# A two-layer diffusion backbone on one core: projections for query, key and value over 512 weight columns at a time, and layer 0's key scores for all x tokens in one pass

## The chip, the cores and the metric

The kernel runs on one core of a Trainium2 chip. The metric is the time of one execution on the device in microseconds (us). The kernel before takes 5148.17 us (median of three runs, 5141.2 to 5151.72).

## What is computed

There are 512 latent tokens (x) and 256 context tokens (ctx), 1024 channels, two layers. Cut to what matters here, each layer does this:

```python
p = xn @ wl                              # one input projection, 10 x 1024 columns; ctx likewise
q = rope(rms(p[..., Q] per 64 columns))  # 8 heads x 2 x 64
k = rope(rms(p[..., K] per 64 columns)); v = p[..., V]
o = softmax(q0 k0) v - lam * softmax(q1 k1) v      # over 768 keys: x and ctx
mix = (g0*rms(o) + g1*pool(p) + g2*conv(p) @ conv_out_w) @ w_out ; h = h + mod*mix
s = (xn2 @ w_q) against 16 tables of 128 keys      # PEER: 8 heads x 2 halves
eidx, gate = top 16 of the sums of two top-16 lists, softmax over them
h = h + mod * sum_k gate*gelu(xn2 . u_emb[eidx]) * v_emb[eidx]   # 128 experts per token
```

Layer 1 needs only the x tokens at its end.

## The kernel before, in words

Every product of two float32 arrays is made of three matmuls in float32r (`mm3`, L96 to L100): both sides are split into a high and a low part (`split`, L91 to L94: a copy on ACT, a subtraction on DVE). Names in the profile: `whi` and `wlo` are the split weights, `hi` and `lo` (or `yh`, `yl` before the FFN) the split activations.

**Projections.** `load_w` (L136) fetches a weight chunk of 1024 x 256 in two DMAs of 512 KB (`wraw`), splits each, and `qkv` (L298) runs, for each pair of heads and each of k, q and v, over token tiles: two token tiles of 256 columns fill one PSUM bank (`qk`), and `qk_tile` normalizes, rotates, splits, transposes and stores them. The token tile is the stationary side of the matmul, the weight columns are what moves. There are 9 chunks of two token tiles for each pair of heads in layer 0 and 8 in layer 1.

**Mixers.** `conv`, `conv_gate`, `conv_out` and `out_proj` run with the weight as the stationary side over 512 tokens. `attn_gate` broadcasts a row of 1/rms to all partitions by a matmul with a selector (`selb`, `hrb`, L494), in float32.

**The FFN has two ways.** For the 512 x tokens of layer 0 (384 in layer 1) all 16384 experts are computed: `keys` scores (`mm<-yh`, `rsc`) and picks the top 16 (MAX8, FIND_INDEX8 and MATCH_REPLACE8 on DVE, `tv`, `ti`, `mr`), `gates` builds a dense gate array (`gA`, `gE`, `gB`, `gps`), `hidden` multiplies by all of u (`ul`, `hid`: 24 matmuls of 512 columns for each split weight tile `ul`, 128 such tiles) and `values` by all of v (`vl`, `dps`). For the 256 ctx tokens of layer 0 (and 128 x tokens of layer 1) `gathered` (L841) fetches the 128 chosen rows of `peer_u` and of `peer_v` for each of 128 tokens by indirect DMAs issued by POOL, 128 x 1024 floats (512 KB) each, into **three buffers** (`row`); DVE multiplies each row (L859, with a sum into `ghid`) or accumulates it (L869, `gacc`). That is 512 rows in layer 0 and 256 in layer 1. Their priority is the lowest of all.

**Order.** The framework's scheduler writes one fixed order of instructions for each engine; each engine then runs its list in that order, and a wait holds up all that is behind it. DVE's list mixes the gathered rows with the splits (`wlo`, `ul`, `vl`) for which TensorE waits. `keys` is called in layer 0 and 1 for two halves of the x tokens, the later half first, which lets the second half's picks start before the first half is scored.

Of the kernel before, what the change touches and what calls it, by code (L numbers as in the profile page):

```python
# [21 lines left out]
F32 = mybir.dt.float32  # L22
# [47 lines left out]
class Net:  # L70
# [227 lines left out]

    def qkv(self, l, streams, kinds):

        nc, a = self.nc, self.a
        with ExitStack() as es:
            ap_ = self.pool(es, f"at{l}{streams[0].i}", 2)
# [3 lines left out]
            for hp in range(NH // 2):  # L307
                for kind in kinds:
                    w = self.load_w(a["w_in"][l, {"q": 0, "k": 4, "v": 8}[kind] + hp], KT, 256)
                    for s in streams:  # L310
                        if l == DEPTH - 1 and s.i and kind == "q":
                            continue
                        for u in range(s.nt // 2):
                            ps = pm.tile([P, 2, 256], F32, tag="mm", name="qk")
                            for t in range(2):
                                for k in range(KT):
                                    xh, xl = s.sub(k, 2 * u + t)
                                    self.mm3(ps[:, t], xh, xl, w[0][k], w[1][k], k == 0, k == KT - 1)
                            if kind == "v":
                                vh = ap_.tile([P, 2, 2, P], F32R, tag="vh", name="vh")  # L320
                                vl = ap_.tile([P, 2, 2, P], F32R, tag="vl", name="vl")
                                pv = ps.rearrange("p t (h c) -> p h t c", h=2)
                                self.split(vh, vl, pv)
                                t0 = (s.t0 + 2 * u) * P
                                for x, v in enumerate((vh, vl)):
                                    for hh in range(2):
                                        nc.scalar.dma_start(self.vd[l][x, 2 * hp + hh][:, t0:t0 + 2 * P],
                                                          v[:, hh].bitcast(F32).rearrange("p t c -> p (t c)"))
                            else:
                                self.qk_tile(l, ap_, pt_, "qk".index(kind), hp, s, u, ps, rot)  # L330

    def qk_tile(self, l, ap_, pt_, i, hp, s, u, ps, rot):
# [3 lines left out]
        psg = ps.rearrange("p t (g c) -> p (t g) c", c=HD)  # L336
# [9 lines left out]
        y4 = y.rearrange("p (t g) c -> p t g c", t=2)  # L346
        z4 = z.rearrange("p (t g) c -> p t g c", t=2)
        if s.i == 0:
            t1 = ap_.tile([P, 8, HD], F32, tag="qt", name="qt")
            t4 = t1.rearrange("p (t g) c -> p t g c", t=2)  # L350
            cx = rc[:, i, 2 * u:2 * u + 2]
            sx = rs[:, i, 2 * u:2 * u + 2]
            nc.vector.tensor_tensor(z4, y4, cx[:, :, None].to_broadcast([P, 2, 4, HD]), op=OP.mult)
            for a_, b_ in ((0, 32), (32, 0)):
                nc.vector.tensor_tensor(t4[:, :, :, a_:a_ + 32], y4[:, :, :, b_:b_ + 32],
                                        sx[:, :, None, a_:a_ + 32].to_broadcast([P, 2, 4, 32]), op=OP.mult)
# [3 lines left out]
        o = (s.t0 + 2 * u) * P  # L360
        st = ap_.tile([P, 2, 2, 2 * P], F32R, tag="st", name="st")
        if i == 0:
# [6 lines left out]
            blk = lambda t, g: zz[:, 2 * t + g // 2, 2 * (g % 2):2 * (g % 2) + 2]  # L369
        else:  # L370
# [5 lines left out]
            blk = lambda t, g: zz[:, 4 * t + g]  # L376
        for t in range(2):
            tr = pt_.tile([P, 4, P], F32R, tag="tr", name="tr")
            for g in range(4):
                nc.tensor.transpose(tr[:, g], blk(t, g).rearrange("p a c -> p (a c)"), self.identr)  # L380
            nc.scalar.activation(st[:, :, :, t * P:(t + 1) * P].rearrange("p h i c -> p (h i) c"), tr, AF.Copy)
        dst = (self.qd, self.kd)[i][l]
        for hh in range(2):
            nc.scalar.dma_start(dst[2 * hp + hh][:, :, o:o + 2 * P], st[:, hh].bitcast(F32))
        if i == 1:
            sl = ap_.tile([P, 2, 2 * P], F32R, tag="sl", name="sl")
            tr = pt_.tile([P, 4, P], F32R, tag="tr", name="tr")
            for hh in range(2):
                for t in range(2):
                    nc.tensor.transpose(tr[:, 2 * hh + t], kl[:, 4 * t + 2 * hh:4 * t + 2 * hh + 2].rearrange("p a c -> p (a c)"), self.identr)  # L390
            nc.scalar.activation(sl.rearrange("p h c -> p (h c)"), tr.rearrange("p a c -> p (a c)"), AF.Copy)
            for hh in range(2):
                nc.scalar.dma_start(self.ld[l][2 * hp + hh][:, o:o + 2 * P], sl[:, hh].bitcast(F32))
# [64 lines left out]
    def attn_gate(self, l, s, pp):  # L458

        nc, a = self.nc, self.a  # L460
        with ExitStack() as es:
# [6 lines left out]
            selb = gp.tile([NH, NH, P], F32, name="selb", bufs=1)  # L468
# [3 lines left out]
            def gate(c):  # L472
                w = self.load_w(a["w_in"][l, 28 + c], KT, 256)
# [14 lines left out]
            R = self.rsqrt_wide(gp, ss, 1.0 / P, [NH, s.n], "hr")  # L488
            for j in range(NH):
# [4 lines left out]
                nc.tensor.matmul(rb, selb[:, j], R, start=True, stop=True)  # L494
# [717 lines left out]
```

## Time and profile before

| | |
|---|---|
| median of three runs | 5148.17 us |
| the profiled execution, its own time | 5138.01 us |
| its span, first to last instruction | 5136.2 us |
| TensorE (PE) busy | 4934.7 us, 96% |
| VectorE (DVE) busy | 3946.9 us, 77% |
| ScalarE (ACT) busy | 1988.4 us, 39% |
| bytes moved | 1280.77 MB, 249 GB/s over the span |

Busy PE time is a union of spans that overlap, since one matmul's span is longer than the distance to the next one's start; how fast PE works is read from the number of matmuls in a stretch. The profiled execution is 10 us shorter than the median of the runs, 1.8 us of its time lie outside the span.

### The profile page before, as it was taken

The numbers are of one execution on the slowest core, as the hardware profiler recorded it, in microseconds if no ns is written. First come the engines' busy times: TensorE is split into PE (matmuls) and PEld (weight loads), VectorE is DVE, ScalarE is ACT, GpSimd is POOL, SyncE is SP. The second block draws the span as 40 slices with busy tenths as digits, with TensorE's granted clock in tenths as the row PEclk, the third lists the DMA queues.
The fourth block names the chain that finished last, engine by engine and source line by source line (L and its number), as shares of the span: only waits on it lengthen the run. The fifth ranks groups of instructions, "written<-read, shape, count | busy, mean of one in ns | idle before, by whom it ended". The sixth has DMA issues, their size and how long they took to land.

```text
span 5136.2 us, 73940 instructions
## 1 busy us (share of the span) xinstructions
PE 4934.7 (96%) x27373; PEld 4195.8 (82%) x27373; DVE 3946.9 (77%) x7993; ACT 1988.4 (39%) x2968; POOL 1180.5 (23%) x1028
## 2 busy tenths in 40 slices
PE   8999999998899999989999999999999999899999
PEld 5688787776688788768888789777679999899999
DVE  5457676697899998568888867666359999787885
ACT  4346664422333344222233234544334344332333
POOL 0001000024433343333333300000000434344320
PEclk9999999999999999999999999999999999999999
DMA  8667453468897889999999845533355888988995
GB/s 305 239 200 224 137 191 108 155 200 273 302 316 259 285 312 339 329 321 326 336 341 344 311 137 166 161 126 97 109 172 174 277 309 331 330 314 294 329 317 177
DMA packets 509035, 1280.77 MB, mean 249 GB/s; under 512 B 42496, under 2 KB 224640, under 8 KB 500352
## 3 DMA queue, kind: packets, MB, share of 16 engines
q1 hardware_dynamic: 302816, 669.35, 38.5%
q0 software_dynamic: 131968, 449.90, 25.7%
q10 hardware_dynamic: 73888, 156.79, 8.1%
q8 instruction: 215, 3.52, 0.3%
q14 instruction: 148, 1.21, 0.1%
HBM read 1098.13 MB, written 177.73 MB: 248 GB/s over the span
## 4 chain that ended last, share of the span: by engine, by line
PE 64%; DMA 14%; DVE 11%; issue 7%; POOL 2%; ACT 1%; SPq 0%; ACTq 0%; POOLq 0%; DVEq 0%
PE mm L98 6%; DMA row<-peer_v,ix 6%; PE mm L100 6%; PE mm L99 6%; DMA row<-peer_u,ix 6%; PE dps L99 5%; PE dps L100 5%; PE dps L98 5%; PE hid L100 4%; PE hid L98 4%; PE hid L99 4%; PE qk L98 3%; PE qk L100 3%; PE qk L99 2%; POOL row L846 2%
## 5 line engine op out<-in xcount | busy, mean ns | idle before, releaser
L100 PE MATMUL hid<-yh,ul 128*128 128x512 f32 (+1 forms) x2048 | 760.2, 372 | 33.9 <-DVE ul L94 33.6
L98 PE MATMUL hid<-yh,uh 128*128 128x512 f32 (+1 forms) x2048 | 757.1, 370 | 21.0 <-ACT yh L286 13.2
L846 POOL DMA_INDIRECT row<-peer_v,ix x384 | 568.5, 1480 | 876.7 <-DVE gacc L869 501.1
L846 POOL DMA_INDIRECT row<-peer_u,ix x384 | 521.4, 1358 | 1059.7 <-DVE row L859 617.7
L99 PE MATMUL hid<-yl,uh 128*128 128x512 f32 (+1 forms) x2048 | 755.7, 369 | 2.3 <-DVE yl L287 2.3
L98 PE MATMUL dps<-wh,vh 128*128 128x512 f32 (+1 forms) x2048 | 735.1, 365 | 20.0 <-ACT vh L93 18.6
L99 PE MATMUL dps<-wl,vh 128*128 128x512 f32 (+1 forms) x2048 | 741.7, 365 | 12.3 <-DVE wl L94 12.3
L100 PE MATMUL dps<-wh,vl 128*128 128x512 f32 (+1 forms) x2048 | 742.0, 364 | 10.4 <-DVE vl L94 10.4
L98 PE MATMUL mm<-hi,whi 128*128 128x512 f32 (+1 forms) x1856 | 666.5, 360 | 12.3 <-DVE y L582 3.1
L100 PE MATMUL mm<-hi,wlo 128*128 128x512 f32 (+1 forms) x1856 | 660.6, 358 | 14.0 <-DVE wlo L94 14.0
L99 PE MATMUL mm<-lo,whi 128*128 128x512 f32 (+1 forms) x1856 | 662.4, 357 | 3.5 <-DVE lo L94 3.5
L859 DVE SCALAR_TENSOR_TENSOR row<-row,gx 128x1024 f32<-128x1024 f32 x384 | 467.0, 1221 | 170.3 <-DMA row<-peer_u,ix 169.5
L869 DVE SCALAR_TENSOR_TENSOR gacc<-row,gw,gacc 128x1024 f32<-128x1024 f32 x381 | 488.1, 1281 | 133.7 <-DMA row<-peer_v,ix 132.6
L94 DVE TENSOR_TENSOR wlo<-wraw,whi 128x1024 fp32r<-128x1024 f32 (+1 forms) x356 | 427.2, 1202 | 179.6 <-ACT whi L93 177.2
L93 ACT ACTIVATE uh<-uraw 128x1024 fp32r<-128x1024 f32 x256 | 271.5, 1061 | 716.4 <-PE hid L99 651.9
L93 ACT ACTIVATE whi<-wraw 128x1024 fp32r<-128x1024 f32 (+1 forms) x356 | 370.5, 1043 | 404.4 <-PE mm L99 305.2
L93 ACT ACTIVATE vh<-vraw 128x1024 fp32r<-128x1024 f32 x256 | 270.2, 1058 | 641.9 <-PE dps L99 395.1
L100 PEld LDWEIGHTS hid<-yh,ul 128*128 128x128 f32 x2048 | 390.2, 191 | 82.9 <-DVE ul L94 44.6
L98 PEld LDWEIGHTS hid<-yh,uh 128*128 128x128 f32 x2048 | 391.1, 191 | 64.1 <-ACT yh L286 15.6
L98 PEld LDWEIGHTS dps<-wh,vh 128*128 128x128 f32 x2048 | 386.7, 189 | 61.9 <-ACT vh L93 19.4
L99 PEld LDWEIGHTS dps<-wl,vh 128*128 128x128 f32 x2048 | 387.1, 189 | 54.8 <-DVE wl L94 14.4
L100 PEld LDWEIGHTS dps<-wh,vl 128*128 128x128 f32 x2048 | 387.2, 189 | 51.5 <-DVE vl L94 11.1
(332 smaller groups left out, 9480.4 us busy)
## 6 DMA issues: line engine op xcount, KB each, us to landing
uraw<-uT SPq DMA_DIRECT2D x256, 512.0 KB, 5.7
vraw<-v SPq DMA_DIRECT2D x256, 512.0 KB, 6.8
wraw<-w_in SPq DMA_DIRECT2D x216, 512.0 KB, 4.4
gd<-gst ACTq DMA_DIRECT2D x28, 2048.0 KB, 10.7
mw<-w_mod SPq DMA_DIRECT2D x96, 512.0 KB, 7.0
wraw<-wq SPq DMA_DIRECT2D x80, 512.0 KB, 6.0
hidd<-ge ACTq DMA_DIRECT2D x128, 256.0 KB, 5.6
G<-gd SPq DMA_DIRECT2D x32, 1024.0 KB, 10.7
```

Source lines behind the costliest of these rows:

```text
L93: self.nc.scalar.activation(hi, src, AF.Copy)
L94: self.nc.vector.tensor_tensor(lo, src, hi.bitcast(F32), op=OP.subtract)
L98: mm(ps, lh, rh, start=start, stop=False)
L99: mm(ps, lh, rl, start=False, stop=False)
L100: mm(ps, ll, rh, start=False, stop=stop)
L846: nc.gpsimd.indirect_dma_start(out=r, out_offset=None, in_=a[t], in_offset=bass.IndirectOffsetOnAxis(ap=idx[:, s:s + 1], axis=0))
L859: nc.vector.scalar_tensor_tensor(out=r, in0=r, scalar=1.0, in1=x, op0=OP.mult, op1=OP.mult, accum_out=hid[:, k:k + 1])
L869: nc.vector.scalar_tensor_tensor(acc, r, w[:, k:k + 1], acc, op0=OP.mult, op1=OP.add)
```

## The change

Four things change.

1. `qkv` takes weight chunks of 1024 x 512 (four heads). `load_wide` fetches one in four DMAs of 512 KB, and its split tiles alternate between a pool of their own (`wq`, three buffers) and the shared one. One token tile of 512 columns now fills a PSUM bank, with 24 matmuls of 512 columns instead of 48 of 256 for two token tiles of half the width. What `qk_tile` computes for a bank is as much as before; the stores of a pair of token tiles are merged into two DMAs (three for k).
2. Layer 0 calls `keys` once for all 512 x tokens. Layer 1 still calls it twice.
3. `attn_gate` splits the 1/rms row and broadcasts it by two float32r matmuls in place of one in float32.
4. The weight array is cut differently in memory (`w_qkv` beside `w_in`), so chunk numbers shift.

```diff
+    def load_wide(self, src, wq):
+        hi, lo = [], []
+        for k0 in range(0, KT, 2):
+            raw = self.wpool.tile([P, 2, 512], F32, tag="wraw", name="wraw", bufs=3)
+            self.nc.sync.dma_start(raw, src[:, k0 * 512:(k0 + 2) * 512].rearrange("p (k c) -> p k c", c=512))
+            pool, n = (wq, 3) if k0 // 2 % 2 else (self.wpool, self.wbufs)
+            h = pool.tile([P, 2, 512], F32R, tag="whi", name="whi", bufs=n)
+            lw = pool.tile([P, 2, 512], F32R, tag="wlo", name="wlo", bufs=n)
+            self.split(h, lw, raw)
...
-            for hp in range(NH // 2):
+            for hg in range(2):
...
-                    w = self.load_w(a["w_in"][l, {"q": 0, "k": 4, "v": 8}[kind] + hp], KT, 256)
+                    w = self.load_wide(a["w_qkv"][l, {"q": 0, "k": 2, "v": 4}[kind] + hg], wq)
...
-                            ps = pm.tile([P, 2, 256], F32, tag="mm", name="qk")
                             for t in range(2):
+                                ps = pm.tile([P, 512], F32, tag="mm", name="qk")
                                 for k in range(KT):
                                     xh, xl = s.sub(k, 2 * u + t)
-                                    self.mm3(ps[:, t], xh, xl, w[0][k], w[1][k], k == 0, k == KT - 1)
+                                    self.mm3(ps, xh, xl, w[0][k], w[1][k], k == 0, k == KT - 1)
...
+            rh = gp.tile([NH, s.n], F32R, name="hrh", bufs=1)
+            rl = gp.tile([NH, s.n], F32R, name="hrl", bufs=1)
+            self.split(rh, rl, R)
...
-                nc.tensor.matmul(rb, selb[:, j], R, start=True, stop=True)
+                nc.tensor.matmul(rb, selb[:, j], rh, start=True, stop=False)
+                nc.tensor.matmul(rb, selb[:, j], rl, start=False, stop=True)
...
-                for t0 in (XT // 2, 0):
-                    y = Stream(0, XT // 2 * P, 0)
-                    y.h, y.l = (x[:, :, t0 * P:t0 * P + y.n] for x in (Y.h, Y.l))
+                for t0, t1 in ((XT // 2, XT), (0, XT // 2)) if l else ((0, XT),):
+                    y = Stream(0, (t1 - t0) * P, 0)
+                    y.h, y.l = (x[:, :, t0 * P:t1 * P] for x in (Y.h, Y.l))
```

The scheduler writes a new order for the whole program. Three places follow, all in DVE's list of layer 0.

The first is where `conv` of the x tokens begins (`z` is its first product). In the kernel before, DVE still picks experts for ctx there:

```order
L94 TENSOR_TENSOR wlo<-wraw,whi 128x1024
L687 TENSOR_SCALAR ri<-pos 128x128
L688 TENSOR_SCALAR ci<-pos 128x128
L679 TENSOR_REDUCE gz<-ge 128x8
L572 TENSOR_TENSOR z<-mm,z 128x512
L630 MAX top<-cand 128x8 x8
L691 CAST rf<-ri 128x128
L692 CAST cf<-ci 128x128
L680 RECIPROCAL gz<-gz 128x8
L572 TENSOR_TENSOR z<-mm,z 128x512
```

In the changed kernel the gathered rows are already running at the same place:

```order
L94 TENSOR_TENSOR wlo<-wraw,whi 128x1024
L872 SCALAR_TENSOR_TENSOR row,ghid<-row,gx 128x1024
L726 TENSOR_TENSOR pk_10969<-eq 128x128
L872 SCALAR_TENSOR_TENSOR row,ghid<-row,gx 128x1024 x2
L94 TENSOR_TENSOR wlo<-wraw,whi 128x1024
L1025 SCALAR_TENSOR_TENSOR ix_10971<-pk_10961,pk_10969 128x128
L585 TENSOR_TENSOR z<-mm,z 128x512 x2
L872 SCALAR_TENSOR_TENSOR row,ghid<-row,gx 128x1024
L94 TENSOR_TENSOR wlo<-wraw,whi 128x1024
L588 SCALAR_TENSOR_TENSOR y<-z,cols,y 128x512 x2
```

The gather moved ahead: it starts 14 weight splits (`wlo`) earlier than it did.

The second is where the x tokens are scored, with `hidden` already running beside it. Before, from one `ul` to the next:

```order
L94 TENSOR_TENSOR ul<-uraw,uh 128x1024
L869 SCALAR_TENSOR_TENSOR gacc<-row,gw,gacc 128x1024
L634 MAX tv_14967<-mr 128x8
L635 MAX_INDEX ti_14970<-tv_14966,mr 128x8
L709 TENSOR_TENSOR eq<-eq,tf 128x2048
L631 MAX_INDEX ti_14970<-tv_14966,rsc 128x8
L634 MAX top<-mr 128x8 x2
L630 MAX tv_14967<-rsc 128x8
L869 SCALAR_TENSOR_TENSOR gacc<-row,gw,gacc 128x1024
L635 MAX_INDEX ti_14971<-tv_14967,mr 128x8
L633 MATCH_REPLACE mr<-tv_14966,rsc 128x128
L711 TENSOR_TENSOR eq<-eq 128x1024
```

And in the changed kernel, up to the next `ul`:

```order
L872 SCALAR_TENSOR_TENSOR row,ghid<-row,gx 128x1024
L644 MAX_INDEX ti_14022<-tv_14018,rsc 128x8
L646 MATCH_REPLACE mr<-tv_14018,rsc 128x128
L872 SCALAR_TENSOR_TENSOR row,ghid<-row,gx 128x1024
L647 MAX tv_14017<-mr 128x8
L647 MAX tv_14018<-mr 128x8
L872 SCALAR_TENSOR_TENSOR row,ghid<-row,gx 128x1024
L648 MAX_INDEX ti_14021<-tv_14017,mr 128x8
L648 MAX_INDEX ti_14022<-tv_14018,mr 128x8
L643 MAX tv_14019<-rsc 128x8
L94 TENSOR_TENSOR ul<-uraw,uh 128x1024
L872 SCALAR_TENSOR_TENSOR row,ghid<-row,gx 128x1024
```

The rows stand closer, and the picks (`eq`, `top`) that stood among the scores of the second half are gone from here; they now come after all scores. Counted over DVE's whole list, the gathered rows stand like this (before, now): between the 143rd and the 192nd `wlo` 93, 123; between the 10th and the 28th `ul` 40, 68; from there to the 46th 36, 36; from there to the last 127, 120; and in `values`, between the 16th and the 88th `vl`, 111, 111. TensorE's list for the 18 `ul` from the 10th holds 192 `mm` of 512 columns and 36 `rsc` besides the 432 `hid` matmuls now, and for the 18 after them next to nothing else. The picks for ctx, on which the gather waits, now lie ahead of the 143rd `wlo`.

The third is the end of layer 0. Before, the last tile of the gather (`gres`) closes the layer, just ahead of the next layer's norm (`nrm`):

```order
L875 SCALAR_TENSOR_TENSOR gres<-gtr,modT_98,gres 128x128
L831 TENSOR_TENSOR acc<-dps,acc 128x512
L835 SCALAR_TENSOR_TENSOR acc<-acc,modT_98,fh 128x512
L875 SCALAR_TENSOR_TENSOR gres<-gtr,modT_98,gres 128x128 x2
L94 TENSOR_TENSOR wlo<-wraw,whi 128x1024 x3
L123 TENSOR_SCALAR nrm<-nps 128x512
L127 TENSOR_TENSOR nrt<-nry 128x256 x2
```

In the changed kernel it is done some 36 of the 128 `vl` earlier:

```order
L844 TENSOR_TENSOR acc<-dps,acc 128x512
L848 SCALAR_TENSOR_TENSOR acc<-acc,modT_98,fh 128x512
L94 TENSOR_TENSOR wlo<-wraw,whi 128x1024 x2
L123 TENSOR_SCALAR nrm<-nps 128x512
L123 TENSOR_SCALAR nrm<-nps 128x256
L127 TENSOR_TENSOR nrt<-nry 128x256 x2
```

What moved is the whole gather of layer 0, towards its start. Layer 1's lists after its projections differ in a few places only.

## Rows read from the trace of the kernel before

**Rows 1.** The page: engines' busy time, and engines on the chain that ended last.
```profile
PE 4934.7 (96%) x27373; PEld 4195.8 (82%) x27373; DVE 3946.9 (77%) x7993; ACT 1988.4 (39%) x2968; POOL 1180.5 (23%) x1028
...
PE 64%; DMA 14%; DVE 11%; issue 7%; POOL 2%; ACT 1%; SPq 0%; ACTq 0%; POOLq 0%; DVEq 0%
```

**Rows 2.** Timeline of PE in layer 0's projections: start, span.
```profile
144.07 0.28 PE L100 MATMUL qk<-whi,lo 128*128 128x256 f32 x1
144.19 0.28 PE L98 MATMUL qk<-whi,hi 128*128 128x256 f32 x1
...
146.11 0.28 PE L99 MATMUL qk<-wlo,hi 128*128 128x256 f32 x1
```

**Rows 3.** Stretch table of tile `dps` alone: stretch, length, PE, PEld, DVE; clock, DMA, GB/s.
```profile
2515.00:2580.00 65.00, 65.00 (x289) 53.83 (x288) 8.61 (x13) 1.00 0.98 341
```

**Rows 4.** Stretch table, values: PE, PEld, DVE, ACT, POOL busy; clock, DMA share, GB/s.
```profile
2305.00:2925.00 620.00, 620.00 (x2735) 513.17 (x2734) 543.62 (x720) 183.22 (x232) 229.51 (x172) 1.00 0.96 336
```

**Rows 5.** The same table from the x mixers to the end of `hidden`.
```profile
1000.50:1087.90 87.40, 87.40 (x427) 71.67 (x426) 82.26 (x338) 24.88 (x32) 6.71 (x10) 1.00 0.33 109
1087.90:1362.90 275.00, 235.56 (x954) 182.18 (x953) 212.79 (x279) 78.19 (x98) 122.58 (x103) 0.95 0.82 281
...
1453.40:1605.40 152.00, 148.80 (x824) 129.14 (x823) 145.39 (x494) 53.45 (x71) 42.09 (x40) 0.99 0.85 288
1605.40:1734.70 129.30, 120.27 (x644) 98.64 (x644) 119.53 (x315) 39.08 (x64) 53.63 (x38) 0.99 0.80 269
1734.70:2253.10 518.40, 509.24 (x2894) 416.08 (x2894) 414.58 (x646) 193.51 (x297) 192.51 (x124) 0.99 0.90 322
```

**Rows 6.** Two of these stretches, tile `row` alone: DVE, then POOL's issues.
```profile
1087.90:1362.90 275.00, 116.00 (x141) 120.10 (x94) 0.95 0.82 281
...
1453.40:1605.40 152.00, 50.29 (x56) 42.09 (x40) 0.99 0.85 288
```

**Rows 7.** Tile `row` from 1085 to 1345: instructions (min/median/max ns), landing.
```profile
L859 DVE SCALAR_TENSOR_TENSOR row<-row,gx x48: 1209/1224/1278, 1092.1 to 1317.5; 128x1024 f32<-128x1024 f32 x48
...
DMA to landing us min/median/max: 4.4/6.2/9.4
```

**Rows 8.** Who waited for whom, 1085 to 1345: total, times, longest.
```profile
POOL row L846 <- DVE row L859: 61.4, 39, 3.9
...
DVE row L859 <- DMA row<-peer_u,ix: 30.0, 21, 2.9
...
PE mm L100 <- DVE wlo L94: 13.5, 9, 3.2
```

**Rows 9.** Groups of PE by shape: count, busy, mean ns, idle before.
```profile
L98 PE MATMUL qk<-whi,hi 128*128 128x256 f32 x1088 | 312.5, 288 | 5.6 <-DVE qy L344 2.2 <-ACT hi L286 1.9 <-DVE nt L285 1.6
...
L98 PE MATMUL mm<-yh,whi 128*128 128x256 f32 x512 | 147.3, 288 | 0.0
...
L494 PE MATMUL hrb<-hry,selb 8*128 8x512 f32 x32 | 18.4, 700 | 4.1 <-DVE hry L133 4.1
...
L494 PE MATMUL hrb<-hry,selb 8*128 8x256 f32 x16 | 6.3, 490 | 1.2 <-ACT rg L476 1.2
```

**Rows 10.** The stretch table in the projections of layers 0 and 1.
```profile
0.00:384.00 384.00, 367.08 (x2522) 266.28 (x2522) 205.36 (x600) 146.27 (x233) 13.22 (x46) 0.99 0.72 249
...
3066.00:3196.00 130.00, 130.00 (x1119) 130.00 (x1119) 91.64 (x271) 54.24 (x78) 0.00 (x0) 1.00 0.47 153
```

**Rows 11.** Chain that ended last, between layers: start, length, what.
```profile
2986.80 1.72 PE nps L275 x4
...
2990.09 3.99 DMA hout<-gres
2994.13 4.74 DMA h<-hout
...
2999.36 2.09 PE nps L275 x4
...
3007.90 0.58 PE qk L98
```

More of the change, by code (lines that the diff above doesn't have):

```diff
@@ L296, in norm @@
                 nc.scalar.dma_start(rows.rearrange("(q p) d -> p q d", p=P), nrow)
+    def load_wide(self, src, wq):
[7 more added lines that the diff above has]
+            self.split(h, lw, raw)
+            for k in range(2):
+                hi.append(h[:, k])
+                lo.append(lw[:, k])
+        return hi, lo
     def qkv(self, l, streams, kinds):
@@ L302, in qkv @@
         with ExitStack() as es:
+            wq = self.pool(es, f"wq{l}{streams[0].i}")
             ap_ = self.pool(es, f"at{l}{streams[0].i}", 2)
@@ L313, in qkv @@
                         for u in range(s.nt // 2):
-                            ps = pm.tile([P, 2, 256], F32, tag="mm", name="qk")
+                            c = slice((s.t0 + 2 * u) * P, (s.t0 + 2 * u + 2) * P)
+                            st = ap_.tile([P, 2, 4, 2, P], F32R, tag="st", name="st")
+                            sl = ap_.tile([P, 4, 2, P], F32R, tag="sl", name="sl") if kind == "k" else None
                             for t in range(2):
+                                ps = pm.tile([P, 512], F32, tag="mm", name="qk")
@@ L316, in qkv @@
                                 for k in range(KT):
                                     xh, xl = s.sub(k, 2 * u + t)
-                                    self.mm3(ps[:, t], xh, xl, w[0][k], w[1][k], k == 0, k == KT - 1)
[L319 to L330, printed above, removed]
@@ L332, in qk_tile @@
-    def qk_tile(self, l, ap_, pt_, i, hp, s, u, ps, rot):
+                                    self.mm3(ps, xh, xl, w[0][k], w[1][k], k == 0, k == KT - 1)
+                                if kind == "v":
+                                    self.split(st[:, 0, :, t], st[:, 1, :, t], ps.rearrange("p (h c) -> p h c", h=4))
+                                else:
+                                    self.qk_tile(l, ap_, pt_, "qk".index(kind), s, 2 * u + t, t, ps, rot, st, sl)
+                            for x in range(2):
+                                src = st[:, x].bitcast(F32).rearrange("p h t c -> p h (t c)")
+                                if kind == "v":
+                                    dst = self.vd[l][x, H][:, :, c]
+                                else:
+                                    dst = (self.qd, self.kd)["qk".index(kind)][l][H][:, :, x, c]
+                                nc.scalar.dma_start(dst.rearrange("h p c -> p h c"), src)
@@ L334, in qk_tile @@
+                            if kind == "k":
+                                nc.scalar.dma_start(self.ld[l][H][:, :, c].rearrange("h p c -> p h c"),
+                                                    sl.bitcast(F32).rearrange("p h t c -> p h (t c)"))
+    def qk_tile(self, l, ap_, pt_, i, s, u, t, ps, rot, st, sl):
         nc = self.nc
         rc, rs, gains = rot
-        psg = ps.rearrange("p t (g c) -> p (t g) c", c=HD)
+        psg = ps.rearrange("p (g c) -> p g c", c=HD)
         sq = ap_.tile([P, 8, HD], F32, tag="qt", name="sq")
@@ L375, in qk_tile @@
             nc.vector.tensor_tensor(kl, z, zz[:, :, 0].bitcast(F32), op=OP.subtract)
-            blk = lambda t, g: zz[:, 4 * t + g]
-        for t in range(2):
+            blk = lambda h, x: zz[:, 2 * h + x]
+        for x in range(2):
             tr = pt_.tile([P, 4, P], F32R, tag="tr", name="tr")
[L379 to L384, printed above, removed]
+            for h in range(4):
+                nc.tensor.transpose(tr[:, h], blk(h, x).rearrange("p a c -> p (a c)"), self.identr)
+            nc.scalar.activation(st[:, x, :, t], tr, AF.Copy)
         if i == 1:
-            sl = ap_.tile([P, 2, 2 * P], F32R, tag="sl", name="sl")
             tr = pt_.tile([P, 4, P], F32R, tag="tr", name="tr")
[L388 to L393, printed above, removed]
+            for h in range(4):
+                nc.tensor.transpose(tr[:, h], kl[:, 2 * h:2 * h + 2].rearrange("p a c -> p (a c)"), self.identr)
+            nc.scalar.activation(sl[:, :, t], tr, AF.Copy)
     def attend(self, l, es, parts, side=None):
@@ L1170, in layouts @@
     r["w_mod"] = chunk(I["w_mod"], 12, KT, 512)
-    r["w_in"] = chunk(I["w_in"], 40, KT, 256)
+    r["w_qkv"] = chunk(I["w_in"][:, :, :3 * D], 6, KT, 512)
+    r["w_in"] = chunk(I["w_in"][:, :, 3 * D:], 28, KT, 256)
     r["conv_out_w"] = chunk(I["conv_out_w"], 4, KT, 256)
```

32 lines of the change are left out of this document (13 added, 19 removed).

## The prediction

> **What bounds the kernel now.** I read the page first. TensorE is busy for 96% of the span, but the chain of waits gives only 64% to it and 14% to DMA, 11% to VectorE [rows 1]. Busy time overlaps itself, so I counted how far apart matmuls start. In the projections 18 matmuls of 256 columns start from 144.07 to 146.11: 2.04 / 17 = 0.120 us each [rows 2]. A matmul of 512 columns takes 65.00 / 289 = 0.225 us [rows 3], and 620.0 / 2735 = 0.227 over the whole values stage, where TensorE never pauses [rows 4]; I use 0.2265. So a pair of 256 costs 0.240, and one of 512 saves 13.5 ns against it.
>
> Where TensorE does pause decides the rest. The stretch table has one bad place: from 1087.9 to 1362.9 TensorE is busy for 235.6 of 275 us [rows 5]. There the gather's rows pass: DVE multiplies 94 of them, one in 275 / 94 = 2.93 us, and POOL's issues of them are in that stretch too [rows 6]. A row takes 1.22 us on DVE and lands 6.2 us (median, 9.4 at most) after its issue [rows 7]. POOL waits for DVE to free a buffer 39 times, 61.4 us in all, DVE waits for a landing 30.0 us, and TensorE waits for `wlo`, which stands behind such rows in DVE's list [rows 8]. Three buffers share one cycle of landing and multiplication, so rows have a pace of their own: (6.2 + 1.22) / 3 = 2.47 us if nothing lies between them, 2.93 as measured with all hand-offs. I take 2.8, nearer to what was measured, because issue and semaphores do cost something. **A stretch whose list holds n rows lasts at least 2.8 n, whatever TensorE has to do.**
>
> **The change, part by part.**
>
> *Projections.* 1088 matmuls per line, three lines, of 256 columns [rows 9]: 3264 x 0.120 = 391.7 us. Now 1632 x 0.2265 = 369.6: -22. In layer 1 TensorE works without a pause and DVE and ACT are busy 91.6 and 54.2 of 130 us [rows 10], their work for a bank is the same, so the gain comes through. In layer 0 TensorE works 367 of 384 us with DMA at 0.72 [rows 10]; a wait could take some of it. I take -21, between 0 (only if each weight chunk, now twice as large, is late by what it saved) and -22.
>
> *Stores and weights.* I cost them at nothing. A bank's 24 matmuls last 5.4 us, in which ACT works 54.24 x 5.4 / 130 = 2.3 us and DVE 3.8 [rows 10]; the merged stores are issued from ACT in the 3.1 us that are left, and bytes and copies per bank stay as they are. Weights come as often per column as before, four tiles for a chunk that lasts twice as long, on SP's queue with nothing else in front. If that cover went, each of the 12 chunks of the two layers would make TensorE wait for one split, 1.2 us of DVE, 15 us in all, which is most of the bound of 0 above.
>
> *Broadcast.* 48 records of `hrb` in float32 take 18.4 + 6.3 us [rows 9]; as 32 matmuls of 512 and 16 of 256 in float32r at the spacings above, 7.2 + 1.9. That is -15.6, of which up to two thirds can be hidden or eaten by the split that now stands ahead of it (one copy and one subtraction for each gate, TensorE behind them): the x gate of layer 0 lies where the rows set the pace. I take -5, from 0 to -11.
>
> *Keys.* 768 of the 1536 `mm` matmuls of 256 columns [rows 9] become 384 of 512: 92.2 to 87.0 us. It lies in the stretches below and is counted there, as are the 16 weight chunks that are no longer fetched and split twice. What matters more is what the new order does with the gather, since DVE's list is fixed and each row in it holds up `ul` and `wlo` behind it.
>
> *x mixers, 143rd to 192nd `wlo`.* Now 87.4 + 275.0 = 362.4 us [rows 5] with 93 rows; 123 in the new list: 123 x 2.8 = 344. The picks for ctx, with which DVE is busy 82.3 of the first 87.4 us now [rows 5], stand ahead; I let the list come about a quarter of them late, 22 us. 344 + 22 - 362 = +4. Bounds: -18 without the lateness, +20 at 2.93 us.
>
> *10th to 28th `ul`.* Now 152.0 us [rows 5] with 40 rows, 42.1 us of POOL's time [rows 6]. The new list has 68: 68 x 2.8 = 190, against what TensorE needs there, (432 + 192) x 0.2265 = 141 and 36 small `rsc`, 148 in all. So the rows set the end: +38. Bounds: -4 (TensorE alone), +47 at 2.93.
>
> *28th to 46th `ul`.* Now 129.3 us [rows 5]. The second half's scores and picks are gone; 432 x 0.2265 = 98 for TensorE and near 100 with what little else is there, 36 x 2.8 = 101 for the rows: -28. Bounds -29 and -24.
>
> *Rest of `hidden`.* Work doesn't vanish: TensorE is busy 148.8 + 120.3 = 269 us in the two stretches now [rows 5], needs 148 + 98 then, and the keys account for 5 of the difference. Some 16 us (gates that come later) move into this rest, which is busy 509 of 518 [rows 5], at fewer rows (127 to 120): +8, from 0 to +16.
>
> *Values.* 111 rows before and after over the same 72 `vl`, one in 3.6 us (620 / 172) [rows 4], DMA share 0.96, TensorE without a pause: 0. Only the last 36 `vl` lose their rows, and nothing waited for those.
>
> *Between the layers.* The chain runs through `hout<-gres`, 3.99 us, and `h<-hout`, 4.74 us, after the last `nps` of x [rows 11]. With `gres` long done, both can leave the chain. I take -5 (ctx's norm must still pass behind something), from 0 to -9.
>
> **Sum**, against the profiled execution's own 5138.0 us: -21 - 5 + 4 + 38 - 28 + 8 + 0 - 5 = -9, 5129. The median of the runs is 10 us above that execution, so 5139 on its scale; I say 5140. A measurement of this kernel can tell some 0.2%, 10 us, from no change: below 5138 counts as faster, above 5158 as slower.
>
> The size of the bets: of the +38 and +4, 2.8 us is the uncertain factor. Each 0.1 us on it moves the total by some 20 us.
>
> **Rivals.**
>
> *B, the rows do not hold up `ul` or `wlo`.* Their pace is 2.6 us or less. For it: landing was 4.4 us at best [rows 7], and a longer `ul` stretch spreads its weight fetches thinner. At 2.6: x mixers 320 + 22 - 362 = -20, `ul` 177 - 152 = +25, then -29: -21 - 5 - 20 + 25 - 29 + 8 - 5 = -47, 5101 on the median's scale; down to 5080 if the pace never shows. Against it: [rows 6] and [rows 8] show this very limit, with TensorE at 86%.
>
> The Trainium skill, "DMA: Bandwidth & Descriptors", section "Anatomy of one DMA — SWDGE (gpsimd) path", gives 2.0 us plus bytes over 436e3, an estimate of 3.2 us for such a row of 512 KB. By that the cycle would be (3.2 + 1.22) / 3 = 1.5 us and this rival would hold. The landings of 4.4 to 9.4 us in [rows 7] do not agree with it.
>
> *C, slower: the denser list runs at 2.93 us or above.* The `ul` stretch fetches weights beside the rows (DMA 0.85 with 40 rows [rows 5]); with 68 the landing could rise above its 6.2 us. At 2.93: +20, +47, -24 in place of +4, +38, -28, so 29 more in all, 5169; at 3.1: +41, +59, -17, so 5209. It decides at about 2.9. Against it: the longer stretch spreads the same weight fetches, so its bytes per us need not rise; and 2.93 had the x mixers' waits in it.
>
> *D, the wide matmul isn't cheaper than its two halves.* Then -21 and the 5 of the keys are gone: 5140 + 26 = 5166. Against it are the two spacings that I read directly [rows 2, 3]; for it, only that no 512-column `qk` is in the trace.
>
> The Trainium skill, "TensorE: Matmul & The Clock Gate", section "Back-to-back issue gap", speaks against the change: its isolated gap is N / 2.4 + 2.5 ns, so two of 256 cost 218.3 and one of 512 costs 215.8, only 2.5 ns saved and, as an estimate, 4 us over 1632 matmuls. By that the sum would be 5161 (17 and 4 of the two savings gone). The trace's 0.120 and 0.2265 [rows 2, 3] differ from it by 10 ns each, which is a saving of 13.5.
>
> **How the numbers follow.** A, as forecast, pace 2.7 to 2.9: 0.45, with 5120 to 5165; of that 0.20 falls below 5138, 0.17 within, 0.08 above. B, 0.28, all faster. C, 0.20, and D, 0.07, slower. So faster 0.48, same 0.17, slower 0.35. The range of 8 in 10 reaches into B (5097) and into C (5188).
>
> **What would show it.** Projections right: TensorE's `qk` at 0.226 us spacing, 544 records per line instead of 1088, and layer 1's projections 10 us shorter. Gather right: from the 10th to the 28th `ul` some 190 us with TensorE idle a fifth of it, waiting for `ul` on DVE, and POOL waiting for DVE's rows; 28th to 46th near 100 us. If that first stretch takes 150 us, B; if 205, C. Between the layers: no `hout<-gres` on the chain. The forecast fails if rows are limited otherwise than by three buffers, or if the picks that moved ahead hold up TensorE before the 143rd `wlo`, which I priced at 22 us of lateness only.

## The result

The changed kernel is **slower**: 5226.15 us median (5222.99 to 5249.43) against 5149.86 us for the kernel before, ratio 1.0161, interval 1.0130 to 1.0193. The prediction said 5140 us and a range up to 5188. The profiled execution has a span of 5221.2 us, 85.0 more than before.

The page of the changed kernel, the lines that answer to [rows 1]:

```profile
PE 4939.3 (95%) x25357; PEld 4094.2 (78%) x25357; DVE 3934.8 (75%) x7980; ACT 1974.2 (38%) x2941; POOL 1142.4 (22%) x1028
...
PE 24%; issue 7%; DMA 4%; DVE 4%; POOL 1%; ACT 1%; POOLq 0%; DVEq 0%; ACTq 0%
```

The shares of this chain add up to 41% of the span, so the profile does not follow it back to the start, and they can't be set beside the 64% of before.

TensorE is as busy as before although it has 2016 fewer matmul records: what it saved is filled with longer spans and lower clocks, and with pauses. The busy share hides all of this; the stretches show it. Each stage below runs from the end of the one above to the first start of a tile or, where it says "last", to the end of that tile's last matmul, in us of one profiled execution of each kernel:

| stretch | before | changed | difference | forecast |
|---|---|---|---|---|
| start to last `qk`, layer 0 | 367.6 | 344.0 | -23.6 | -11 |
| to the first `ul` (all mixers) | 967.4 | 1034.5 | **+67.1** | +4, and part of -5 |
| 1st to 10th `ul` | 118.4 | 114.9 | -3.5 | 0 |
| 10th to 28th | 152.0 | 186.1 | **+34.1** | +38 |
| 28th to 46th | 129.3 | 115.8 | -13.5 | -28 |
| 46th to 128th | 526.0 | 528.3 | +2.3 | +8 |
| to the last `dps`, layer 0 | 726.1 | 722.8 | -3.3 | 0 |
| to the first `qk`, layer 1 | 21.1 | 17.8 | -3.3 | -5 |
| first to last `qk`, layer 1 | 209.7 | 219.5 | **+9.8** | -10 |
| to the first `hid`, layer 1 | 606.2 | 614.6 | +8.4 | part of -5 |
| to the end | 1312.4 | 1322.9 | +10.5 | 0 |

The largest loss lies in the mixers, where the x gate begins. The stretch table of the changed kernel there (PE, PEld, DVE, ACT, POOL; clock, DMA share, GB/s), which answers to the first row of [rows 5]:

```profile
980.00:1000.00 20.00, 14.06 (x63) 8.02 (x61) 19.45 (x127) 4.73 (x8) 2.36 (x10) 0.83 0.01 3
1000.00:1020.00 20.00, 6.07 (x8) 0.80 (x8) 20.00 (x123) 4.71 (x8) 0.00 (x0) 0.68 0.00 0
1020.00:1040.00 20.00, 18.78 (x63) 13.51 (x64) 17.38 (x53) 6.71 (x8) 7.70 (x5) 0.81 0.29 83
1040.00:1060.00 20.00, 15.65 (x57) 11.13 (x57) 19.30 (x30) 3.21 (x4) 7.79 (x6) 0.87 0.93 325
```

And who waited for whom from 980 to 1060 (total, times, longest):

```profile
POOL row L859 <- DVE gg L695: 43.3, 1, 43.3
...
PE hrb L506 <- ACT hrh L93: 9.4, 1, 9.4
ACT osq L495 <- PE hss L496: 9.2, 4, 5.5
```

From 1000 to 1020 DVE works without a pause through 123 small instructions, the picks for ctx, while TensorE has 8 matmuls and the DMA engines nothing. The granted clock falls to 0.68, a mean of 20 us at its two levels (1.2 and 2.4 GHz), after those pauses. In the kernel before TensorE is busy for all of 87.4 us there.

The stall is one part of the loss. The two lines below are the changed kernel, from the 143rd `wlo` to the first gathered row and from there to the first `ul`; the two after them are the same stretches of the kernel before:

```profile
980.00:1036.10 56.10, 35.30 (x121) 19.89 (x120) 52.97 (x293) 14.61 (x22) 8.91 (x13) 0.76 0.05 14
1036.10:1378.50 342.40, 301.56 (x1226) 234.97 (x1224) 262.69 (x341) 85.66 (x107) 152.16 (x135) 0.96 0.84 287
```

```profile
1000.50:1092.10 91.60, 91.60 (x445) 75.13 (x444) 83.53 (x340) 25.61 (x33) 9.55 (x14) 1.00 0.35 117
1092.10:1335.00 242.90, 213.79 (x890) 168.32 (x888) 186.61 (x242) 64.43 (x80) 107.62 (x93) 0.98 0.83 282
```

TensorE stands still for 20.8 us of the first stretch, where it did not pause before. In the second it stands still for 40.8 us instead of 29.1, and the stretch is 99.5 us longer: 118 rows pass there instead of 85, and matmuls that covered the picks before are done there (1226 records instead of 890).

Elsewhere: the gathered rows in the mixers and in two `ul` stretches (tile `row` alone: DVE, then POOL's issues), then all instructions of the `ul` stretches:

```profile
1100.00:1360.00 260.00, 116.15 (x141) 116.42 (x93) 0.97 0.83 282
1493.40:1679.50 186.10, 85.15 (x100) 71.20 (x68) 0.98 0.85 282
1679.50:1795.30 115.80, 44.75 (x54) 40.14 (x36) 0.99 0.87 291
```

```profile
1493.40:1679.50 186.10, 164.53 (x714) 128.73 (x713) 156.85 (x435) 39.76 (x53) 71.20 (x68) 0.98 0.85 282
1679.50:1795.30 115.80, 106.58 (x466) 86.44 (x465) 104.23 (x338) 33.31 (x44) 41.68 (x37) 0.99 0.87 291
```

The first `ul` stretch holds 68 rows at 186.1 / 68 = 2.74 us, these 260 us of the mixers 93 at 260 / 93 = 2.80. Over the whole of the prediction's own stretch, from the first row to the start of the 193rd `wlo`, rows come more slowly, one in 368.5 / 125 = 2.95 us (tile `row` alone):

```profile
1036.10:1404.60 368.50, 157.00 (x190) 159.45 (x125) 0.94 0.83 286
```

And who waited for whom from 1493.4 to 1679.5, the first `ul` stretch:

```profile
PE rsc L664 <- DVE mr L646: 16.4, 13, 2.4
PE hid L100 <- DVE ul L94: 4.0, 2, 3.8
...
DVE row L872 <- DMA row<-peer_u,ix: 14.7, 15, 2.8
DVE gacc L882 <- DMA row<-peer_v,ix: 14.2, 12, 3.4
```

DVE's 156.85 us of work and these 28.9 us of waiting for rows make 185.8 of the 186.1: DVE's list sets the length of this stretch, and rows are 85.15 us of its work.

TensorE's `qk` by shape answers to [rows 9] (count, busy, mean ns, idle before), and layer 1's projections to the second row of [rows 10]:

```profile
L98 PE MATMUL qk<-whi,hi 128*128 128x512 f32 x544 | 219.7, 405 | 22.9 <-ACT whi L93 9.8 <-ACT hi L286 8.6 <-DVE qy L367 4.5
...
L100 PE MATMUL qk<-whi,lo 128*128 128x512 f32 x544 | 215.4, 397 | 0.0
```

```profile
3063.00:3284.00 221.00, 202.80 (x979) 166.97 (x980) 160.84 (x447) 95.95 (x144) 0.21 (x4) 0.95 0.43 142
```

22.9 us of idle time stand before these matmuls instead of 5.6. 9.8 us of it is one wait in layer 1 for `whi` on ACT.

### The profile page after: what moved, and what is told of

Read it like the earlier page. It is cut to its first block, busy times and chain, and to the rows that moved or that the text cites. A ratio compares the mean times of both kernels' runs of the same rounds, so it can differ in the third digit from the quotient of the medians.

```text
span 5221.2 us, 69583 instructions
## 1 busy us (share of the span) xinstructions
PE 4939.3 (95%) x25357; PEld 4094.2 (78%) x25357; DVE 3934.8 (75%) x7980; ACT 1974.2 (38%) x2941; POOL 1142.4 (22%) x1028
## 5 line engine op out<-in xcount | busy, mean ns | idle before, releaser
L98 PE MATMUL dps<-wh,vh 128*128 128x512 f32 (+1 forms) x2048 | 736.8, 365 | 10.7 <-ACT vh L93 7.1
L859 POOL DMA_INDIRECT row<-peer_u,ix x384 | 503.6, 1312 | 1083.1 <-DVE row L872 600.3
L859 POOL DMA_INDIRECT row<-peer_v,ix x384 | 548.0, 1427 | 848.4 <-DVE gacc L882 442.6
L93 ACT ACTIVATE uh<-uraw 128x1024 fp32r<-128x1024 f32 x256 | 271.3, 1060 | 770.4 <-PE hid L99 699.1
L94 DVE TENSOR_TENSOR wlo<-wraw,whi 128x1024 fp32r<-128x1024 f32 (+1 forms) x340 | 407.5, 1201 | 192.1 <-ACT whi L93 184.7
L93 ACT ACTIVATE whi<-wraw 128x1024 fp32r<-128x1024 f32 (+1 forms) x340 | 352.7, 1043 | 403.0 <-PE mm L99 310.8
L99 PEld LDWEIGHTS hid<-yl,uh 128*128 128x128 f32 x2048 | 391.6, 191 | 43.9 <-DVE yl L287 4.0
```

The costliest lines, as they stand in the source:

```text
L93: self.nc.scalar.activation(hi, src, AF.Copy)
L94: self.nc.vector.tensor_tensor(lo, src, hi.bitcast(F32), op=OP.subtract)
L98: mm(ps, lh, rh, start=start, stop=False)
L99: mm(ps, lh, rl, start=False, stop=False)
L859: nc.gpsimd.indirect_dma_start(out=r, out_offset=None, in_=a[t], in_offset=bass.IndirectOffsetOnAxis(ap=idx[:, s:s + 1], axis=0))
```

## The experiments

Three theories stood at the outset. **T**: the two new tiles of the gate's split (`hrh`, `hrl`, 8 x 512 each, in a pool that reserves 2 KB per partition for each) are the cause: the pool no longer fits where it did, the x gate waits for memory that the picks for ctx hold, and the scheduler puts all picks and the gather ahead of it. **K**: the keys in one pass move the gather. **Q**: the wide projections do it by their buffers. All ratios are to the kernel before. Stages of a run are read from its one profiled execution; executions of one kernel differ by some 40 us (23 of the kernel before, 5127 to 5168 us).

**One edit undone, and the same edit in other memory.** The first kernel takes the gate's split out of the changed kernel:

```diff
-            self.split(rh, rl, R)
-                nc.tensor.matmul(rb, selb[:, j], rh, start=True, stop=False)
-                nc.tensor.matmul(rb, selb[:, j], rl, start=False, stop=True)
+                nc.tensor.matmul(rb, selb[:, j], R, start=True, stop=True)
```

> The changed kernel with one edit undone: the gates broadcast 1/rms by one float32 matmul again. Theory T: the two tiles hrh and hrl make the gates' pool larger, so the x gate of layer 0 has to wait for memory that the picks for ctx hold; the scheduler puts all those picks and the gather ahead of it, and this made the 73 us that were lost between the 120th and the 152nd wlo and what the 10th to 28th ul lost. Then this kernel takes 5115 to 5140 us. Rival Q (the wide projections make the loss by their buffers and the order they lead to): 5215 or more. Rival K (the keys in one pass move the gather): 5215 or more.

Measured: 1.0084 (1.0064 to 1.0103), 5185 us. The first `ul` comes at 1336.6 us, 1.6 us from before and 42 earlier than in the changed kernel. But it is still slower than before: T's range ends 45 us lower, and Q and K, with 5215 or more, miss too.

The second keeps the split and puts both tiles into buffers that exist:

```diff
-            rh = gp.tile([NH, s.n], F32R, name="hrh", bufs=1)
-            rl = gp.tile([NH, s.n], F32R, name="hrl", bufs=1)
+            rh = gp.tile([P, s.n], F32R, tag="osq", name="hrh")[:NH]
+            rl = gp.tile([P, s.n], F32R, tag="osq", name="hrl")[:NH]
```

> The changed kernel with all its edits, but hrh and hrl take the two buffers of osq, which are free by then, so the pool is as large as before. T: 5110 to 5140 us, within 10 us of the kernel without the split, and hss of the x gate no longer waits behind the picks. If the split itself (two more steps ahead of hrb) is what costs, it stays above 5200, and hrb still waits some 9 us for hrh. Q and K: 5215 or more.

Measured: 1.0049 (1.0031 to 1.0067). 0.0112, 58 us, are gone with the same instructions, the first `ul` at 1326.1. T holds for the mixers, but the 5163 us lie above its range: 0.5% is left that T doesn't explain.

**Each edit alone on the kernel before.** The split as in the change:

> The kernel before with this one edit alone (split 1/rms, two float32r matmuls, two new tiles). T: 5205 to 5235 us. Q and K: 5140 to 5150, since neither the projections nor the keys are touched.

Measured: 1.0128 (1.0108 to 1.0148), 5203 us, the first `ul` 71 us late. Neither projections nor keys are touched, so Q and K can't be all. T gave 5205 to 5235 and misses by 2 us.

The wide projections alone:

> The wide projections alone (keys in two halves, the gate in float32 as before). T: the forecast's 21 us less what the start of layer 1's projections lost (some 20 us of waits for the norm of ctx and for the third weight tile): 5130 to 5150 us. If keys in one pass gain 5 us or more, this is that much slower than the kernel with the gate's edit alone undone. Q: 5200 or more.

Measured: 1.0100 (1.0082 to 1.0118), 5195 us, 45 above T's range and 5 short of Q's: 52 us slower, not level. The loss is not in layer 0, where the last `dps` is 6.8 us later than before, but in layer 1: 50 us.

**Where the wide projections lose.** In every kernel whose layer 0 is wide the first scores (`sc`) start 14.7 to 15.3 us after the last `qk`, 0.8 without; in layer 1 it is 14.3 against 1.3 to 3.1 (and 19.5 and 21.1 in the two kernels below with the fills on DVE). I put this down to zero fills of pooling and conv that stand ahead of attention's first loads on POOL's queue:

```diff
-                        nc.gpsimd.memset(u[:, 0:8], 0.0)
+                        nc.vector.memset(u[:, 0:8], 0.0)
```

(and three more like it.)

> The kernel with all edits and the gates' tiles in osq's buffers, in which the two zero fills of pooling (pu) and of conv (z) are made by DVE instead of POOL. Theory W: the wide projections' larger pools make these fills wait for the last qk, they stand ahead of attention's first loads (hq) on POOL's in-order queue, and so the first scores come 14 us (layer 0) and 13 us (layer 1) after the last qk, not 0.5 and 1.3 as before; attention is the longest chain of the mixers, so its end has no other work beside it. Then hq is issued before the last qk in both layers and the time falls by 15 to 28 us, to 5135 to 5148. Rival V (the wide projections lose only at the start of layer 1, by the norm and the third weight tile): no change, 5157 to 5167.

Measured: 1.0066 (1.0045 to 1.0086), no gain; 5175 us lie above V's range too. The loads now start 35 us before the last `qk` of layer 0 (309.9 against 344.5), and the first scores still come 14.7 us after it. This theory is wrong: TensorE's own list puts other matmuls (`mm`, and the last `mps`) ahead of the scores, it does not pause before them, and no load is late.

Next, the layers apart, each with the old projections in the other one and the gate's tiles in `osq`:

> All edits, gates' tiles in osq's buffers, but layer 1 projects in chunks of 256 columns as before. Both W and V: layer 1's loss of 22 us (from the first qk of layer 1 to the end, against before) goes, 5135 to 5145. If layer 1's loss comes from layer 0 (the order of the gather, the clock), the time stays at 5157 to 5167.

Measured: 1.0028 (1.0013 to 1.0043), against 1.0049 with both; 5155 us, between the two expectations.

> The counterpart: wide projections in layer 1 alone, all else as in the kernel with the gates' tiles in osq's buffers. W: layer 1's first scores come 13 us after its last qk, and layer 1 takes 20 us longer than before; layer 0 gains nothing from the projections and loses nothing at attention's start: 5150 to 5170. V: the same in layer 1, so these two are told apart by the first qk of layer 1: 10 us earlier than in the kernel with both layers wide if W's loss in layer 0 is as large as its gain there, 10 to 20 us later if layer 0 loses nothing.

Measured: 1.0091 (1.0071 to 1.0111), slower than with both layers wide and above the expected 5150 to 5170. The first `qk` of layer 1 comes 18.8 us later than with both: layer 0's wide projections do pay there. On the base below, with keys in halves, they don't: 0.9994 against 0.9972.

The last of this group gives the first chunk of layer 1 three tiles from the shared pool, which is free earlier:

```diff
+            pool, n = (wq, 3) if (k0 == 6 if first else k0 // 2 % 2) else (self.wpool, self.wbufs)
```

> As the kernel with the fills on DVE, and the first weight chunk of layer 1 takes three of its four split tiles from the shared pool, whose buffers are free earlier. V: TensorE's gap of 9.8 us before the third tile at layer 1's start goes to under 5 us, and the time falls by 5 to 10 us against the kernel with the fills alone. W alone: no difference beyond 5 us.

Measured: 1.0061 (1.0039 to 1.0082), level with the kernel without it, though TensorE's wait for `whi` is 0.9 us instead of 10.3 and the first to the last `qk` takes 212.2 instead of 218.7 us. The gain of V is there in the stretch and not in the total.

**The base.** The kernel before with the split alone, its tiles in `osq`:

> The kernel before with the gates' split alone, its two tiles in osq's buffers. The instructions are those of the kernel with the split alone (1.0128 of before); only the place of two tiles differs. T (memory): 0.997 to 1.001 of before, the x gate stays where it was, and 5 to 10 us of TensorE's time are gained. If the split's steps cost something themselves: 1.005 or more.

Measured: **0.9972 (0.9959 to 0.9985)**, 5131.24 us: faster than both kernels. With the same instructions in new memory it was 1.0128, so the place of two small tiles is worth 1.6%, some 80 us. The stretch table of this kernel where the changed one stalls:

```profile
1000.00:1020.00 20.00, 20.00 (x128) 17.50 (x128) 16.29 (x65) 5.24 (x8) 0.00 (x0) 1.00 0.36 121
1020.00:1040.00 20.00, 20.00 (x101) 16.24 (x100) 18.02 (x68) 4.92 (x7) 2.15 (x5) 1.00 0.32 107
```

DVE has the same picks to do, but `mm` matmuls lie beside them.

**The keys alone, and three parts together.**

> The kernel before with the keys of layer 0 in one pass alone. Theory K2 (the denser gather sets the end from the 10th to the 28th ul, 66 rows in 175 to 190 us, and the next 18 ul give 20 us back): 10 to 20 us slower than before, 1.002 to 1.004. Rival (the keys cost nothing beyond their 5 us less TensorE work): 0.998 to 1.000.

Measured: 1.0076 (1.0062 to 1.0090), 5187 us, twice the loss that K2 gave. From the 10th to the 28th `ul` it takes 180.8 us, and 116.8 to the 46th: +28.8, as expected, and -12.5 where 20 were to come back. 24 us more are lost in `hidden` of layer 1, in a profile that is the slowest of the kernel's executions, 16 us above their median.

> Wide projections in layer 0 alone, the gates' split in osq's buffers, keys in two halves: the three parts that should not lose. If the keys in one pass cost the 10 to 20 us of K2: that much less than the same kernel with the keys in one pass (1.0028 of before), 0.998 to 1.001. If not: 1.002 to 1.004.

Measured: 0.9994 (0.9981 to 1.0007). 0.0034, 17 us, less than with the keys in one pass, as K2 said.

**The rows' pace.** Two buffers instead of three:

```diff
-            r = gp.tile([P, D], F32, tag="row", name="row", bufs=3)
+            r = gp.tile([P, D], F32, tag="row", name="row", bufs=2)
```

> The kernel with all edits and the gates' tiles in osq's buffers, with two buffers for the gathered rows instead of three. If three buffers sharing one cycle of issue, landing and product set the pace (2.74 us a row there), two give 4.1 us a row: 52 rows between the 10th and the 28th ul in the new list, 205 to 220 us. If the DMA engines' bandwidth or POOL's issue sets it, the pace stays near 2.8 and the stretch is TensorE's 150 us.

Measured: 1.0725 (1.0706 to 1.0744). The stretch table, tile `row` alone, of the 10th to the 28th `ul` and of 200 us in the x mixers:

```profile
1478.50:1655.70 177.20, 65.35 (x75) 52.03 (x52) 0.98 0.74 240
...
1130.00:1330.00 200.00, 68.88 (x78) 66.02 (x54) 0.94 0.69 237
```

In the x mixers a row takes 200 / 54 = 3.70 us with two buffers and 2.80 with three: the buffers' cycle sets the pace there. It is not half as much again (4.20), and the landing fell with it, to 5.2 us (median) from the 6.2 of [rows 7]. In the `ul` stretch it is 177.2 / 52 = 3.41, not 4.1, a miss: DVE is busy there for 147.1 us and waits 29.5 for rows, so its list fills that stretch with two buffers as with three, and the scores' own work has a large share in it. Of the 356 us that are lost against three buffers, 157 lie at the end of layer 0, where TensorE waits for the gather's tail (175.0 us from the last `dps` to the first `qk` instead of 18.2).

**What was still open, one part at a time on the base.** First, nothing but the memory, in the kernel before:

```diff
+            for x in "hl":
+                nc.vector.memset(gp.tile([NH, s.n], F32, name="hr" + x, bufs=1)[:, 0:1], 0.0)
```

> The kernel before, float32 gate and all, with two more tiles of 8 x 512 in the gates' pool, of which one column is zeroed and nothing read. Theory T (the memory alone puts the x gate behind all ctx picks): 1.010 to 1.016 of before, 60 to 75 us lost up to the first ul, as with the split in new memory. If the split's instructions had a part in it: under 1.005.

Measured: 1.0132 (1.0105 to 1.0160), the first `ul` 70 us late, as T said. Its stretch table at the x gate:

```profile
1000.00:1020.00 20.00, 9.71 (x33) 4.26 (x31) 19.79 (x146) 3.71 (x6) 0.96 (x10) 0.75 0.00 0
1020.00:1040.00 20.00, 11.04 (x15) 2.27 (x15) 20.00 (x101) 6.63 (x10) 0.00 (x0) 0.67 0.00 0
```

The stall of the changed kernel is there, with float32 gates, old projections and keys in halves: DVE full, TensorE with 33 and 15 matmuls, no DMA, the clock at 0.75 and 0.67. The memory alone makes it.

> The base (before with the split in osq's buffers, 0.9972) with the keys of layer 0 in one pass. Its list has 68 rows between the 10th and the 28th ul. K2: 25 to 35 us longer there, 12 to 20 us given back up to the 46th, so 10 to 20 us slower than the base: 0.999 to 1.001. If the 39 us of the run with the keys alone are the keys' own: 1.004 or more.

Measured: 1.0037 (1.0022 to 1.0053), between the two expectations. The two `ul` stretches, first in this kernel and then in the base:

```profile
1448.20:1636.30 188.10, 171.49 (x738) 137.66 (x736) 156.10 (x433) 41.72 (x56) 76.55 (x69) 0.95 0.85 281
1636.30:1750.20 113.90, 104.35 (x443) 84.48 (x444) 102.34 (x329) 30.19 (x40) 40.21 (x38) 0.96 0.86 287
```

```profile
1452.40:1607.90 155.50, 148.30 (x826) 128.59 (x825) 146.98 (x498) 54.42 (x72) 50.24 (x42) 1.00 0.82 284
1607.90:1737.20 129.30, 118.94 (x636) 96.76 (x635) 117.58 (x311) 37.22 (x62) 56.68 (x38) 0.99 0.78 262
```

+32.6 and -15.4. Beyond these, the projections of layer 1 take 215 us instead of 204.4 and its `hidden` 916.8 instead of 903.1 (first to last `hid`). Of the 10.7 us in the projections 7.7 are no loss: the first `qk` comes 17.5 us after the last `dps` instead of 25.2.

> The base with wide projections in layer 1 alone, keys in halves. If TensorE's gap of 10 us before the third weight tile and the later first scores are what layer 1's wide chunks cost: first to last qk 217 to 221 us instead of 209, and the whole 10 to 25 us slower than the base, 0.999 to 1.002. If the forecast's 10 us gain came through: 0.995 or less.

Measured: 1.0031 (1.0016 to 1.0047), 0.6% slower than the base. First to last `qk` 212.7 us, below the expected 217 to 221, against 204.4. Who waited for whom there, from 3005 to 3070:

```profile
PE qk L98 <- ACT whi L93: 5.2, 1, 5.2
```

The first scores come 14.3 us after the last `qk`, attention's last `po` 445.7 us after it (433.9 in the base), and the stretch from the last `qk` to the first `hid` is 615.3 instead of 602.3 us.

## Why the prediction was wrong

**Broadcast: the step that failed first.** I counted the matmuls and the two steps of the split, and gave nothing to the tiles that hold its result. The gain itself was there. In the base `hrb` is busy for 7.3 + 6.3 + 3.1 + 2.6 = 19.3 us:

```profile
L497 PE MATMUL hrb<-hrh,selb 8*128 8x512 f32 x16 | 7.3, 475 | 5.1 <-ACT hrh L93 5.1
L498 PE MATMUL hrb<-hrl,selb 8*128 8x512 f32 x16 | 6.3, 412 | 0.0
...
L497 PE MATMUL hrb<-hrh,selb 8*128 8x256 f32 x8 | 3.1, 408 | 2.0 <-ACT rg L476 1.6 <-ACT hrh L93 0.3
L498 PE MATMUL hrb<-hrl,selb 8*128 8x256 f32 x8 | 2.6, 347 | 0.0
```

Before it was 24.7 [rows 9]: 5.4 us less, with 7.1 us of waiting in front instead of 5.3. That is close to the 5 that I took. The base as a whole is 0.28% (14 us) faster than before, which `hrb` alone does not account for; the new order has a part in it that I did not trace. But the tiles' memory costs 1.3% by itself, with no use made of them. What is shown is that their place decides where the x gate and the picks stand; that they fall on memory which the picks hold is read from the order and not shown directly. TensorE's list of the changed kernel at this point:

```
4287 L100 MATMUL mm<-hi,wlo 128x256
4288 L664 MATMUL rsc<-keys,rq 128x128 x6
4289 L496 MATMUL hss<-osq,sel 8x512 x8
4290 L506 MATMUL hrb<-hrh,selb 128x512 x2
4291 L98 MATMUL mm<-hi,whi 128x512
```

All eight `hss` of the x gate stand behind the last scores (`rsc`) of ctx. Before, they start from 947.3 to 968.1 us with 96 `mm` matmuls of 256 columns among them, and the last `rsc` comes 60 us later: `mm` matmuls are left to cover the picks.

**x mixers: +4 became +62.** That is the prediction's own stretch, 362.4 us before and 424.6 in the changed kernel (it ends where the 193rd `wlo` starts); over all mixers it is the +67 of the table, of which 14 us are matmuls that now stand between the last `qk` and attention's first scores. Two terms of the sum were too small. The picks were priced as 22 us of lateness on DVE, and the first row came 56.1 us after the 143rd `wlo`: 34 us more. I did not look at what TensorE had beside the picks. It had nearly nothing: the next instructions of its list were `hss`, which wait 7.0 us for squares that stand behind the picks' `ge` in ACT's list, and `hrb`, which wait 9.4 us for `hrh`, and that for DVE. Then 125 rows took 2.95 us each, 368.5 us, where I had 123 x 2.8 = 344: 24 us more. The two bounds, -18 and +20, held the second of these and not the first. The prediction did name the first as what would make it fail, but looked for it ahead of the 143rd `wlo`; the stall lies between the 143rd and the 144th.

**Projections.** Starts of `qk` lie 0.227 us apart (median in both layers; 0.120 before), where I took 0.2265, so rival D is out. In layer 0 that gives 864 x 13 ns = 11 us, the forecast share. Its last `qk` came 21 to 24 us earlier in every wide kernel, but the rest is not the forecast's merit: 14 `mps` matmuls moved behind it, and what else helped is not shown. Nor is it kept: the first scores come 9.7 us earlier than before (358.3 us against 368.1), and attention's last `po` starts at 885.5 instead of 886.1. The step that failed is "the gain comes through" in layer 1. I had one weight split per chunk as the price of a lost cover; in the changed kernel it was a start in which TensorE waits 9.8 us for a split tile of the first chunk, after 7.3 us for the norm, with a clock of 0.67 in the first 20 us; and a later start of attention: on the base 8 us longer projections and 13 us longer mixers, 21 of the 30 us by which that kernel is slower, where I had 10 of gain.

**The rows' pace: right in part, and not for the reason given.** In the mixers it was 2.95 us, as slow as before (2.93), where 2.8 was taken; two buffers slow it further. So B is out there. In the `ul` stretch 68 x 2.8 = 190 came close (+34.1 against +38), but with luck: its length is DVE's work and DVE's waits, of which rows are 85 + 29 of 186 us, and not the cycle of three buffers alone. Nor does TensorE wait there mainly for `ul` (4.0 us) but for `mr` (16.4 us), the picks that free its score buffers, and it stands still for an eighth of the time, not a fifth. C's pace was right in the mixers and its cause was not, since the pace did not rise.

**28th to 46th `ul`: half of the gain.** 115.8 us where I had 101: DVE is busy for 104.23 of it. With 338 instructions, the picks for x are now here, and TensorE waits 9.2 us for `ul` on DVE; I had looked at TensorE and the rows only.

**Between the layers and values** came near what was told: -3.3 each, where -5 and 0 were said.

**What stays open.** In layer 1 every kernel with wide projections or keys in one pass loses more in `hidden` (910 to 930 us from first to last `hid`, 936 with two buffers for the rows, against 900 to 906 in the kernel before, the base and the split alone; 912 with the memory alone), also where layer 1's program is as before. The lists of DVE differ there in where rows and picks stand. I have not shown which difference costs it. The two values of 930 come from profiles that are the slowest executions of their kernels, so a part of this may be the spread between executions. Nor is it settled why TensorE's list puts 14 us of other matmuls ahead of the first scores when projections are wide, nor what these cost: TensorE does not pause for them. The parts do not add: on the base, layer 0 wide, layer 1 wide and the keys cost 0.22, 0.59 and 0.65%, and all three together 0.77%.

## What to carry to other kernels

A tile costs its memory as well as its instructions: where one static plan orders everything, ask for each new tile what its pool now overlaps and look in the order for whose release it waits. When an order moves work of one engine ahead, look at what the others have beside it at that place: the cover that is lost has a price beside the length of what moved. And add up one engine's work and waits over a stretch before a cycle of buffers is made its limit. Reusing a buffer that is idle (here `osq`) kept a gain of 0.3% that two new tiles of 8 rows turned into a loss of 1.3%.

## What was not expected of the hardware

A float32 matmul of 8 rows by 512 columns showed as two records of 700 ns [rows 9]. In float32r the two matmuls that replace it showed as one record each, of 475 and 412 ns in the base.

The landing of a gathered row depends on what else runs. In the two-buffer kernel's tail from 3120 to 3280 us, nearly alone (other queues move 5.5 of 28.5 MB), tile `row` shows

```profile
DMA to landing us min/median/max: 4.0/4.2/10.2
```

where the median was 5.2 us in the same kernel's mixers and 6.2 with three buffers beside the mixers' weights [rows 7]. The fit of the Trainium skill ("DMA: Bandwidth & Descriptors", section "Anatomy of one DMA — SWDGE (gpsimd) path") gives an estimate of 3.2 us for 512 KB. Even nearly alone the trace is 1 us above it.

TensorE's clock came down to a mean of 0.67 and 0.68 in stretches in which it had 8 to 15 matmuls in 20 us. In the changed kernel it stayed at the lower level after the stall had ended, while TensorE was busy without a pause, and fell once more later:

```profile
1022.00:1027.50 5.50, 5.50 (x14) 4.27 (x14) 5.50 (x23) 1.62 (x3) 0.00 (x0) 0.50 0.00 0
1027.60:1054.80 27.20, 23.81 (x96) 17.03 (x95) 23.89 (x44) 6.47 (x9) 14.69 (x9) 1.00 0.70 225
1054.90:1061.60 6.70, 5.56 (x12) 3.97 (x13) 6.70 (x9) 0.00 (x0) 0.94 (x1) 0.50 1.02 396
1061.70:1100.00 38.30, 36.85 (x163) 30.17 (x162) 32.76 (x52) 11.51 (x15) 16.99 (x21) 1.00 0.84 286
```
